# Layout conversion of four neighbourhood-attention outputs: spread over low-rank heads 3 to 6 instead of all at head 6

## The chip, the cores and the metric

The kernel runs on one core of one Trainium2 chip. A time is the device time of one execution in microseconds (us). A core has engines that work side by side, each through its own instructions in order: TensorE (PE, matrix products; its weight loads are shown as PEld), VectorE (DVE), ScalarE (ACT), GpSimd (POOL) and SyncE (SP), which here issues most of the transfers. Engines wait for each other by semaphores. On-chip tiles lie in SBUF, results of PE in PSUM banks.

## The reference, cut to what matters

Two layers of a diffusion backbone over 512 latent tokens (a grid 64 wide) and 256 context tokens, 1024 features. Layer 0 mixes two groups of eight heads each, low-rank (latent) attention and two-dimensional neighbourhood attention, and gives their concatenated outputs to one output projection:

```python
def even_mixer(...):
    ...
    o_mla_lat, o_mla_ctx = mla_heads(p_lat[..., :MLA_IN], p_ctx[..., :MLA_IN], rows, cols,
                                     q_norm, kv_norm, w_q_up, w_uk, w_uv, ctx_out)
    ...
    o_na_lat, o_na_ctx = na_heads(na_l[:, :, 0], na_l[:, :, 1], na_l[:, :, 2],
                                  na_c[:, :, 0], na_c[:, :, 1], na_c[:, :, 2], rel_bias, ctx_out)
    o_lat = jnp.concatenate([o_mla_lat, o_na_lat], axis=-1) @ w_out
    o_ctx = jnp.concatenate([o_mla_ctx, o_na_ctx], axis=-1) @ w_out if ctx_out else None
```

Then `h = h + g_a * o`, a SwiGLU block, and layer 1 (sliding-window attention, SwiGLU). The output is the final norm of the latent tokens. All of it is float32.

## The kernel before

Activations are kept with features on the 128 partitions and all 768 tokens along the row: columns 0 to 511 latent (`LATS`), 512 to 767 context (`CTXS`). A float32 product is made of three matmuls: each operand is split into a high part and the rest, and `mm3` (lines 335, 337, 338) multiplies high × high, high × rest and rest × high. `load_w` (line 319) brings a weight block: a transfer by SP into a `wr` buffer (three of them), the high part by ACT (line 324) into `wh`, the rest by DVE (line 325) into `wl`.

During attention the latent tokens are in an order by half-blocks of the grid. Neighbourhood heads run first, two heads to a pair, and each pair leaves one tile of 128 features × 768 tokens: the list `ON`, four tiles. The low-rank heads 0 to 7 follow, and their pairs leave four more: `OM`. Every pair's tile must be put back in rows of the grid and split into high part and rest before the output projection can use it. `in_rows` (line 1163) does both in one go, with four instructions: on ACT a copy of the latent columns (line 1168) and one of the context columns (1169), which give the high part; on DVE two subtractions (1170, 1171), which give the rest. This is called a conversion below. Conversions of `ON` write into general buffers (tag `b`), those of `OM`, at line 1209 behind the head loop, into buffers of tag `st`. So in the profile a row `b<-b` at line 1168 belongs to the neighbourhood outputs and `st<-b` to the low-rank ones.

One low-rank head is worked like this. PE makes scores (lines 1118 to 1120) into the three `pss` banks; DVE adds and finds the extreme (`take`, line 555) into a tile `p` (every fourth time one of the tag `wr`); ACT takes the exponential (551); PE transposes 128 × 128 blocks (499) into banks `pst` and `psd`; DVE (490) or ACT (491) moves them to SBUF as `ph` and `pl`; PE forms the weighted sums (545) in the one `pso` bank, and ACT copies them to the pair's tile (639). At the end of a pair the sums are inverted (475), spread over the partitions with two transposes (367), and multiplied in (`L482`, DVE). `latent_operands` prepares the next heads: a copy by ACT (1108) and a subtraction by POOL (1109).

The output projection (`output`, from line 1230) goes over eight blocks of 128 output features, first for columns 384 to 767 (`TOK2`), then for the others. For a block, 8 × 3 matmuls of 128 × 384 sum over the eight converted tiles: the four of `ON` first in the list `O`, then the four of `OM`. Its residual is loaded by eight transfers `in_xn` on SP (line 134).

The program is written in one order, and the framework's scheduler sets each engine's order at build time. It simulates a timeline, and takes for each engine the ready instruction with the first claim, by a priority that follows the order in which the instructions were written. So a call written earlier changes where its instructions and those around it stand. `attend` draws jobs from `mla_jobs` one ahead, and the lines after a head's `yield from` run when its jobs have been drawn.

Of the kernel before, what the change touches and what calls it, by code (L numbers as in the profile page):

```python
# [98 lines left out]
def hybrid_kernel(ctx: ExitStack, tc, I, out):  # L99
# [6 lines left out]
    def T(tag, shape, dt=F32):  # L106
        count[0] += 1
        if tag not in SIZES:
            return sb.tile(shape, dt, tag=tag, name=f"{tag}_{count[0]}", bufs=BUFS.get(tag, 1))
        n = int(np.prod(shape[1:]))  # L110
        t = sb.tile([P, SIZES[tag] // (2 if dt == mybir.dt.bfloat16 else 4)], dt, tag=tag, name=f"{tag}_{count[0]}",
                    bufs=BUFS[tag])[: shape[0], :n]
        if len(shape) == 3:
            t = t.rearrange("p (a b) -> p a b", a=shape[1])
        return t

    def B(dt=F32, tag="b"):
        return T(tag, [P, NT], dt)

    def PS(tag):  # L120
        count[0] += 1
        return ps.tile([P, 512], F32, tag=tag, name=f"ps{tag}_{count[0]}", bufs=PBUFS[tag])
# [13 lines left out]
    def f(ap):  # L136
        return ap.bitcast(F32) if ap.dtype == F32R else ap
# [219 lines left out]
    def split(src, eng=None, dst=None):  # L357

        p, n = src.shape
        h, lo = dst or (B(F32R), B(F32R))  # L360
        marks["cast"] = S.copy(h[:p, :n], src)  # L361
        marks["split"] = (eng or V).tensor_tensor(lo[:p, :n], src, f(h[:p, :n]), op=ALU.subtract)
        return h, lo
# [267 lines left out]
    def head_jobs(h, po, then):  # L631

        r = slice(64 * h.side, 64 * h.side + 64)
        for qs in ((4,), (5,)), ((0, 1), (2, 3)):

            def use(o, qs=qs):
                for i, x in enumerate(qs):
                    c = slice(x[0] * P, (x[-1] + 1) * P)
                    S.copy(po[r, c], o[64 * i : 64 * i + 64, : c.stop - c.start])

            yield job([(h, x) for x in qs], use, then if qs[0][0] == 0 else None)
# [20 lines left out]
    def drain(gen=None):  # L662

        while side_work and (gen is None or gen in side_work):
            step()
# [107 lines left out]
    def keys_of(v, side, mixed=None):  # L773

        def get(kt):
            t, i = (v, kt) if kt < 6 else (mixed, kt - 6)
            return t[:, i * P + 64 * side : i * P + 64 * side + 64]

        return get
# [156 lines left out]
    def beside(gen):  # L936
        side_work.append(gen)
        return gen
# [60 lines left out]
    ON, lat_raw, kr = [], [None] * 3, []  # L999
# [31 lines left out]
    def finish(po, sums, nq):  # L1031
        finish_pair(po, sums, nq)
        yield
# [35 lines left out]
    def pair_ups(p):  # L1069
        kn.append(B())  # L1070
        qn.append(B())
        wk = wu["kv"]
        yield from up(cut((wk[0][:, 0:1], wk[1][:, 0:1]), p * P, P), wu["ckv"], put(kn[p]))
        yield from up(cut(wu["qn"], p * P, P), wu["cq"], put(qn[p], scale=MLA_SCALE))
        if p % 2 == VP:
            yield from values(p - VP)
# [16 lines left out]
    def latent_operands(h):  # L1093
        p, s = divmod(h, 2)
        r, u = NOPE[s], USED[s]
        rr = slice(32 * (h % 4), 32 * (h % 4) + 32)
        if p < 2:
            if p == 0:
                KA.append([T("st", [P, NT], F32R) for _ in range(2)])
            QA[s].append([T("st", [P, NT], F32R) for _ in range(2)])  # L1100
            for t in [*(KA[s] if p == 0 else ()), *QA[s][p]] if s else ():
                (V if "z" in EV else G).memset(f(t[:32]), 0.0)
            if p == 0:
                for i in range(2):
                    V.tensor_copy(KA[s][i][ROPE[s]], KR[i][:32])
        (ka, kc), (qa, qb) = KA[s], QA[s][p % 2]
        for x, (hi, lo) in ((kn[p], (ka, kc)), (qn[p], (qa, qb))):
            S.copy(hi[r], x[r])
            (V if "l" in EV and p < 1 else G).tensor_tensor(lo[r], x[r], f(hi[r]), op=ALU.subtract)
        for t, x in zip((qa, qb), QR[h // 4]):  # L1110
            if "d" in EV:
                dma(t[ROPE[s]], x[rr])
            else:
                G.dma_start(t[ROPE[s]], x[rr])

        def scores(o, q, keys):
            q = slice(q * P, (q + 1) * P)
            PE.matmul(o, qa[u, q], ka[u, keys], start=True, stop=False)
            PE.matmul(o, qb[u, q], ka[u, keys], start=False, stop=False)
            PE.matmul(o, qa[u, q], kc[u, keys], start=False, stop=True)  # L1120

        return scores
# [40 lines left out]
    def in_rows(src, dst=None):  # L1163

        h, lo = dst or (B(F32R), B(F32R))
        half_blocks = lambda x: x[:, LATS].rearrange("p (n r c) -> p r n c", n=GW // HB, c=HB)
        rows = lambda x: x[:, LATS].rearrange("p (r n c) -> p r n c", n=GW // HB, c=HB)
        S.copy(rows(h), half_blocks(src))  # L1168
        S.copy(h[:, CTXS], src[:, CTXS])
        V.tensor_tensor(rows(lo), half_blocks(src), rows(f(h)), op=ALU.subtract)  # L1170
        V.tensor_tensor(lo[:, CTXS], src[:, CTXS], f(h[:, CTXS]), op=ALU.subtract)
        return h, lo


    OM, O = [], []

    def mla_jobs():
        phase[0], lower[0] = 1, LOWER
        rate[0] = STEPS[1], BG[0][4]
        ready.append(latent_operands(1))  # L1180
        for h in range(8):
            p, s = divmod(h, 2)
            if s == 0:
                g = beside(pair_ups(p + 1)) if p < 3 else None
                po = B()
                sums, mins = T("sm", [P, 6, 2]), T("sm", [P, 6, 2])
            yield from head_jobs(Head(s, ready[h], keys_of(VM[p], s), lambda n: (0, 4), lambda n: zeros.to_broadcast([P, NL]),
                                      -LOWEST, sums, mins), po, finish(po, sums, 6) if s else None)
            if s == 0 and g:
                drain(g)  # L1190
            if h < 6:
                ready.append(latent_operands(h + 2))
            if h == 6:
                O.extend(in_rows(o) for o in ON)
            if s == 1:
                OM.append(po)

    attend(mla_jobs())
    drain()
    dense[0] = True  # L1200
# [365 lines left out]
    for t0, n in ((0, 4), (4, 2)):  # L1566
        o = PS("t")
# [8 lines left out]
    OS, O = [], []  # L1576
# [36 lines left out]
    O = [split(o[:, LATS], dst=(B(F32R, "st"), B(F32R))) for o in OS]  # L1613
# [179 lines left out]
```

## Time and profile before

| | us |
|---|---|
| runs | 1585.27, 1585.99, 1589.26 |
| median | 1585.99 |
| profiled execution | 1587.13 |
| its span | 1585.4 |
| PE busy | 1531.6 (97% of the span) |
| DVE busy | 1163.0 (73%) |
| ACT busy | 796.2 (50%) |
| POOL busy | 294.7 (19%) |

The granted TensorE clock was 0.994 of full speed. The span runs from the first to the last instruction that the profiler recorded; the execution's own time has a little more around it. In what follows a stretch such as 366–372 is in microseconds from the start of the span. The low-rank heads' work lies before about 390, with the neighbourhood heads ahead of it; the output projection of layer 0 begins to be mixed into it near 370. A row of the timeline gives the start, the length, the engine, the line, the operation, out<-in, and, in brackets, how long the engine was idle before it and what released it. Rows of one line and form that follow each other are put together (x2, x4).

### The profile page before, as it was taken

What the parts mean: (1) busy time and instruction counts of PE and PEld (TensorE: products, weight loads), DVE (VectorE), ACT (ScalarE), POOL (GpSimd) and SP (SyncE); (2) the same over time, 40 slices, a digit from 0 to 9 for tenths busy, and PEclk for the clock granted to TensorE, in tenths of its full rate; (3) what the DMA queues carried; (4) which work ended last, traced back from release to release, by engine and by line L of the source; (5) the groups of instructions that cost most, each with busy time, mean ns of one, the idle gap of its engine ahead of it and who ended that gap; (6) DMA issues with size and microseconds to landing.
All of it is one profiled execution on the core that took longest, in us unless ns stands there. A gap on an engine that the chain in (4) does not pass through costs nothing. (4 is left out here: it accounts for less than half of the span.)

```text
span 1585.4 us, 26553 instructions
## 1 busy us (share of the span) xinstructions
PE 1531.6 (97%) x10024; PEld 1375.6 (87%) x10024; DVE 1163.0 (73%) x2331; ACT 796.2 (50%) x1607; POOL 294.7 (19%) x316
## 2 busy tenths in 40 slices
PE   6999999999999999999999999989999999999998
PEld 4787778877998999998989998878889998899997
DVE  3885787676677696887768666868876778678685
ACT  4563687675555242332323334557756545454453
POOL 0144634210011101111020221492012000000001
PEclk9999999999999999999999998999999999999999
DMA  9745332004444645547475585131015123324222
GB/s 311 253 130 175 86 119 72 16 2 160 165 156 142 197 146 192 189 123 276 139 268 171 173 322 181 42 98 49 1 48 167 54 97 124 103 84 131 88 89 87
DMA packets 76464, 214.91 MB, mean 136 GB/s; under 512 B 9872, under 2 KB 16400, under 8 KB 76336
## 3 DMA queue, kind: packets, MB, share of 16 engines
q1 hardware_dynamic: 59216, 144.42, 28.2%
q0 software_dynamic: 15968, 67.24, 12.3%
q8 instruction: 78, 1.28, 0.3%
q10 hardware_dynamic: 1152, 1.57, 0.3%
q14 instruction: 50, 0.41, 0.1%
HBM read 186.97 MB, written 23.07 MB: 132 GB/s over the span
## 5 line engine op out<-in xcount | busy, mean ns | idle before, releaser
L324 ACT CAST wh<-wr 128x1024 fp32r<-128x1024 f32 (+2 forms) x148 | 115.4, 795 | 207.1 <-PE pss L1377 33.8
L325 DVE TENSOR_TENSOR wl<-wr,wh 128x1024 fp32r<-128x1024 f32 (+2 forms) x145 | 135.5, 942 | 79.8 <-ACT wh L324 79.6
L551 ACT ACTIVATE p<-p,sm 128x512 f32<-128x512 f32 (+3 forms) x144 | 104.9, 729 | 27.1 <-DVE sm L555 25.3
L233 DVE CUSTOM_DVE_ANT_0 p<-rope,cond 128x1024 bf16<-128x1024 f32 x64 | 77.1, 1221 | 47.5 <-DMA rope<-in_mod_w_dram 47.5
L1378 PE MATMUL pss<-b,wl 128*128 128x384 f32 (+1 forms) x346 | 106.9, 312 | 1.7 <-DVE wl L1364 1.7
L1376 PE MATMUL pss<-b,wh 128*128 128x384 f32 (+1 forms) x346 | 107.7, 312 | 0.6 <-ACT b L361 0.6
L1377 PE MATMUL pss<-b,wh 128*128 128x384 f32 (+1 forms) x346 | 107.9, 312 | 0.1
L337 PE MATMUL psd<-b,wh 128*128 128x512 f32 (+3 forms) x262 | 89.7, 342 | 0.0
L335 PE MATMUL psd<-b,wh 128*128 128x512 f32 (+3 forms) x222 | 80.1, 361 | 1.6 <-ACT b L464 1.2
L338 PE MATMUL psd<-b,wl 128*128 128x512 f32 (+3 forms) x222 | 78.5, 355 | 0.0
L545 PE MATMUL pso<-ph,b 128*64 128x256 f32 (+1 forms) x384 | 77.2, 359 | 0.4 <-DVE ph L490 0.4
L545 PE MATMUL pso<-pl,b 128*64 128x256 f32 (+1 forms) x384 | 76.7, 359 | 0.7 <-DVE pl L490 0.7
L1378 PE MATMUL pst<-b,wl 128*128 128x384 f32 (+1 forms) x226 | 70.8, 313 | 3.0 <-DVE wl L1364 3.0
L228 POOL DMA_DIRECT2D rope<-in_mod_w_dram x48 | 25.5, 532 | 244.0 <-DVE mod L233 230.9
L1377 PE MATMUL pst<-b,wh 128*128 128x384 f32 (+1 forms) x226 | 70.5, 312 | 0.0
L1376 PE MATMUL pst<-b,wh 128*128 128x384 f32 (+1 forms) x226 | 70.5, 312 | 0.0
L337 PE MATMUL pss<-b,wh 128*128 128x256 f32 (+3 forms) x216 | 69.6, 322 | 0.1
L1659 POOL TENSOR_TENSOR p<-p,p 128x256 f32<-128x256 f32 x6 | 4.6, 766 | 347.3 <-ACT p L1655 347.2
L335 PE MATMUL pss<-st,wh 128*128 128x512 f32 (+2 forms) x198 | 67.3, 340 | 1.1 <-ACT st L1168 0.8
L1378 PEld LDWEIGHTS pss<-b,wl 128*128 128x128 f32 x346 | 65.4, 190 | 2.5 <-DVE wl L1364 2.2
L338 PE MATMUL pss<-st,wl 128*128 128x512 f32 (+2 forms) x198 | 67.1, 339 | 0.0
L1376 PEld LDWEIGHTS pss<-b,wh 128*128 128x128 f32 x346 | 65.6, 190 | 1.1 <-ACT b L361 0.9
(623 smaller groups left out, 5403.9 us busy)
## 6 DMA issues: line engine op xcount, KB each, us to landing
wr<-in_w_gu_dram SPq DMA_DIRECT2D x88, 512.0 KB, 4.2
rope<-in_mod_w_dram POOLq DMA_DIRECT2D x48, 512.0 KB, 3.8
wr<-in_w_dn_dram SPq DMA_DIRECT2D x73, 256.0 KB, 2.9
wr<-in_w_out_dram SPq DMA_DIRECT2D x32, 512.0 KB, 3.5
p<-home POOLq DMA_DIRECT2D x40, 384.0 KB, 5.4
home<-p POOLq DMA_DIRECT2D x40, 384.0 KB, 4.9
wr<-in_w_in_dram SPq DMA_DIRECT2D x21, 512.0 KB, 4.6
nb<-in_nb_dram SPq DMA_DIRECT2D x16, 384.0 KB, 3.3
```

The costliest lines, as they stand in the source:

```text
L228: G.dma_start(w, I["mod_w"][at])
L233: V.tensor_tensor_reduce(out=T("p", [P, D], mybir.dt.bfloat16), in0=w, in1=cond[:, v, :], op0=ALU.mult, op1=ALU.add, scale=1.0, scalar=0.0 ...
L324: behind(S.copy(h, r), *after[:1])
L325: behind((G if eng else V).tensor_tensor(lo, r, f(h), op=ALU.subtract), *after[1:])
L335: ins = PE.matmul(o, wh[:, k], mh[:, c], start=first and k == 0, stop=False)
L337: PE.matmul(o, wh[:, k], ml[:, c], start=False, stop=False)
L338: PE.matmul(o, wl[:, k], mh[:, c], start=False, stop=last and k == n - 1)
L545: ins = PE.matmul(o[64 * i : 64 * i + 64, c], v(kt), t, start=n == 0, stop=n == len(moving[i]) - 1)
L551: S.activation(p[:, c], p[:, c], AF.Exp, bias=nm, scale=-1.0, accum_out=dn)
L1376: PE.matmul(o, wh, xh, start=first and k == 0, stop=False, skip_group_check=not first)
L1377: PE.matmul(o, wh, xl, start=False, stop=False, skip_group_check=not first)
L1378: PE.matmul(o, wl, xh, start=False, stop=k == 3, skip_group_check=not first)
```

## The change

`mla_jobs` no longer converts all four neighbourhood outputs once head 6 has been drawn. It converts one after each of heads 3, 4, 5 and 6, in the list's order.

```diff
             if h < 6:
                 ready.append(latent_operands(h + 2))
-            if h == 6:
-                O.extend(in_rows(o) for o in ON)
+            if h in (3, 4, 5, 6):
+                O.append(in_rows(ON[len(O)]))
             if s == 1:
                 OM.append(po)
```

The instructions are the same in number and kind. Their order differs in one piece of the program, from head 3 to the start of the output projection.

VectorE, from the end of head 6 into head 7. `b_1822`, `b_1997`, `b_2290` and `b_2627` are the four neighbourhood outputs, `wl_4304` and `wl_4340` the rests of the second and third weight block. Before:

```order
L490 COPY ph_4064<-pst_4059 128x512
L475 RECIPROCAL sm_4202<-sm_3846 128x12
L1170 TENSOR_TENSOR b_4000<-b_1997,b_3999 128x512
L1171 TENSOR_TENSOR b_4000<-b_1997,b_3999 128x256
L1170 TENSOR_TENSOR b_4006<-b_2290,b_4005 128x512
L1171 TENSOR_TENSOR b_4006<-b_2290,b_4005 128x256
L490 COPY ph_4107<-pst_4102 128x512
L325 TENSOR_TENSOR wl_4304<-wr_4301,wh_4303 128x1024
L1170 TENSOR_TENSOR b_4012<-b_2627,b_4011 128x512
L1171 TENSOR_TENSOR b_4012<-b_2627,b_4011 128x256
L490 COPY ph_4158<-psd_4153 128x512
L325 TENSOR_TENSOR wl_4340<-wr_4337,wh_4339 128x1024
```

Now:

```order
L490 COPY ph_4064<-pst_4059 128x512
L475 RECIPROCAL sm_4202<-sm_3864 128x12
L490 COPY ph_4107<-pst_4102 128x512
L490 COPY ph_4158<-psd_4153 128x512
L490 COPY pl_4165<-pst_4160 128x512
L325 TENSOR_TENSOR wl_4304<-wr_4301,wh_4303 128x1024
L490 COPY ph_4172<-pst_4167 128x512
L490 COPY ph_4186<-pst_4181 128x512
L325 TENSOR_TENSOR wl_4340<-wr_4337,wh_4339 128x1024
```

Six subtractions are gone from here. The two weight subtractions stand behind more copies of head 7 than before: `wl_4304` behind `ph_4158` and `pl_4165`, `wl_4340` behind all of them. On TensorE the first block's products up to the last finished low-rank pair now stand together ahead of head 7's first sums; before, most of them came behind these.

ScalarE, at head 5. `b_3528` before and `b_3534` now are the same pair's tile. Before:

```order
L551 ACTIVATE p_3806,sm_3529<-p_3806,sm_3530 128x768
L551 ACTIVATE wr_3825,sm_3529<-wr_3825,sm_3530 128x768
L639 COPY b_3528<-pso_2914 64x128 x2
L1108 CAST st_2915<-b_3552 64x768
L1168 CAST st_4240<-b_3182 128x512
L1169 CAST st_4240<-b_3182 128x256
L551 ACTIVATE p_3835,sm_3529<-p_3835,sm_3530 128x768
```

Now:

```order
L639 COPY b_3534<-pso_2914 64x128 x2
L1168 CAST b_3716<-b_1997 128x512
L1169 CAST b_3716<-b_1997 128x256
L1108 CAST st_2915<-b_3558 64x768
L1168 CAST st_4240<-b_3182 128x512
L1169 CAST st_4240<-b_3182 128x256
L551 ACTIVATE wr_3837,sm_3535<-wr_3837,sm_3536 128x768
L1168 CAST b_3857<-b_2290 128x512
L1169 CAST b_3857<-b_2290 128x256
L551 ACTIVATE p_3847,sm_3535<-p_3847,sm_3536 128x768
```

The second and third neighbourhood output are converted here, the second ahead of the operands' copy (1108) that POOL waits for, the third between two exponentials. The pair of low-rank heads 2 and 3 (`st_4240`) was converted here before too.

TensorE, behind the last head's last weighted sums (`pso_2914`); `pss_4343` is the third output block. Before:

```order
L545 MATMUL pso_2914<-ph_4158,b_3282 64x256
L545 MATMUL pso_2914<-pl_4151,b_3282 64x256
L367 MATMUL pst_4212<-ident_r_86,pl_4213 128x128 x2
L335 MATMUL pss_4343<-st_4240,wh_4339 128x384
L337 MATMUL pss_4343<-st_4241,wh_4339 128x384
L338 MATMUL pss_4343<-st_4240,wl_4340 128x384
L335 MATMUL pss_4343<-st_4246,wh_4339 128x384
L337 MATMUL pss_4343<-st_4247,wh_4339 128x384
L338 MATMUL pss_4343<-st_4246,wl_4340 128x384
L335 MATMUL pss_4272<-st_4252,wh_4268 128x384
```

Now:

```order
L545 MATMUL pso_2914<-ph_4158,b_3282 64x256
L545 MATMUL pso_2914<-pl_4151,b_3282 64x256
L338 MATMUL pss_4343<-b_3528,wl_4340 128x384
L335 MATMUL pss_4343<-b_3716,wh_4339 128x384
L337 MATMUL pss_4343<-b_3717,wh_4339 128x384
L367 MATMUL pst_4212<-ident_r_86,pl_4213 128x128 x2
L338 MATMUL pss_4343<-b_3716,wl_4340 128x384
L335 MATMUL pss_4343<-b_3857,wh_4339 128x384
L337 MATMUL pss_4343<-b_3858,wh_4339 128x384
L338 MATMUL pss_4343<-b_3857,wl_4340 128x384
L335 MATMUL pss_4343<-b_4011,wh_4339 128x384
```

Six products of the third block stood between the last head and the first product that needs its converted output (`st_4252`); now 19 do, eight of them in the rows shown; `b_3528`, `b_3716`, `b_3857` and `b_4011` are here the high parts of the four neighbourhood outputs. On SP, the eight loads `in_xn`, which stood behind the third load of `w_out`, now stand between the first and the second.

## The prediction

> **What bounds the kernel now.** I read the page first: busy time by engine, then the chain that ended last.
>
> ```profile
> span 1585.4 us, 26553 instructions
> PE 1531.6 (97%) x10024; PEld 1375.6 (87%) x10024; DVE 1163.0 (73%) x2331; ACT 796.2 (50%) x1607; POOL 294.7 (19%) x316
> PE 31%; DVE 3%; issue 3%; DMA 3%; POOL 2%; ACT 1%; DVEq 0%; POOLq 0%; ACTq 0%
> ```
>
> PE is busy 97% of the span and holds most of what the chain shows. The change adds and removes no instruction, so it can only win back PE's waits. They total 53.8 us over the whole span (1585.4 − 1531.6), and few of them are near the edit. So I read busy time by stretch next (columns: stretch, length, then PE, PEld, DVE, ACT and POOL busy, PE clock, DMA share, GB/s).
>
> ```profile
> 340.00:350.00 10.00, 9.28 (x69) 7.10 (x69) 8.77 (x23) 6.18 (x16) 1.83 (x1) 1.00 0.00 2
> 366.00:372.00 6.00, 4.37 (x27) 2.76 (x26) 6.00 (x11) 5.98 (x14) 0.00 (x0) 1.00 0.32 87
> 390.00:400.00 10.00, 8.28 (x44) 6.13 (x41) 7.60 (x14) 5.96 (x10) 0.00 (x0) 1.00 0.14 29
> ```
>
> Two places matter. In 366–372, after head 6, where all four conversions stand, DVE (6.00 of 6) and ACT (5.98) are full and PE is short by 1.63 us. In 390–400, where the low-rank heads hand over to the output projection, PE is short by 1.72 us. At 340–350, where two of the conversions go, DVE has 1.23 us left.
>
> **The change, part by part. The price of one conversion.** ACT's timeline around head 6 (start, length, instruction, the wait before it in brackets); `b<-b` rows at L1168 and L1169 are conversions of neighbourhood outputs, `st<-b` rows those of low-rank outputs, which stay:
>
> ```profile
> 366.13 0.62 ACT L1168 CAST b<-b 128x512 fp32r<-128x512 f32 x1
> 366.96 0.62 ACT L1168 CAST st<-b 128x512 fp32r<-128x512 f32 x1
> 369.66 0.61 ACT L1168 CAST b<-b 128x512 fp32r<-128x512 f32 x1
> 370.59 0.59 ACT L491 COPY pl<-pst 128x512 f32<-128x512 f32 x1
> ```
>
> From one conversion's start to the next instruction's, 366.13 to 366.96, is 0.83 us of ACT. DVE's timeline there:
>
> ```profile
> 368.46 0.68 DVE L1170 TENSOR_TENSOR b<-b,b 128x512 fp32r<-128x512 f32 x1
> 369.39 0.68 DVE L1170 TENSOR_TENSOR st<-b,st 128x512 fp32r<-128x512 f32 x1
> 370.33 0.68 DVE L490 COPY pl<-psd 128x512 f32<-128x512 f32 x1
> 370.93 1.21 DVE L325 TENSOR_TENSOR wl<-wr,wh 128x1024 fp32r<-128x1024 f32 x1
> ```
>
> By the same reading, 368.46 to 369.39 is 0.93 us of DVE. Three of the four leave: 3 × 0.83 = 2.5 us of ACT and 3 × 0.93 = 2.8 us of DVE. The fourth output (`ON[3]`) is still converted after head 6, just where the first one stood, so up to about 370 us both engines run as before.
>
> **Term 1, start of the tail.** PE's timeline:
>
> ```profile
> 367.40 0.33 PE L499 MATMUL pst<-ident_r,wr 128*128 128x128 f32 x1 [0.58 <-DVE ph L490]
> 371.07 0.65 PE L545 MATMUL pso<-pl,b 128*64 128x256 f32 x2 [0.71 <-DVE pl L490]
> 372.13 0.60 PE L499 MATMUL pst<-ident_r,p 128*128 128x128 f32 x4
> 372.49 0.42 PE L338 MATMUL pss<-b,wl 128*128 128x384 f32 x1
> ```
>
> The four transposes at 372.13 (0.36 us until L338 starts) need the PSUM bank that ACT's L491 copy at 370.59 empties. That copy stands behind a departing conversion (369.66, until 370.59). Without it the transposes fit into the 0.71 us gap ahead of 371.07, and L338 starts at about 372.13, held then by DVE's L325 (370.93 + 1.21 = 372.14). Gain 0.36; bounds 0 and 0.71, the whole gap. The earlier wait of 0.58 stays, since DVE's rows ahead of it are the same.
>
> **Term 2, end of the tail.** The last low-rank head's output takes a copy, a normalisation and its own conversion before PE may use it (timelines of PE, ACT and DVE):
>
> ```profile
> 390.48 0.38 PE L545 MATMUL pso<-pl,b 128*64 128x256 f32 x1
> 390.79 0.44 PE L367 MATMUL pst<-ident_r,pl 128*128 128x128 f32 x2
> 391.94 0.34 PE L338 MATMUL pss<-st,wl 128*128 128x384 f32 x1
> 393.08 0.44 PE L335 MATMUL pss<-st,wh 128*128 128x384 f32 x1 [0.80 <-ACT st L1168]
> ...
> 390.91 0.74 ACT L639 COPY b<-pso 64x256 f32<-64x256 f32 x2 [5.94 <-PE pso L545]
> ...
> 391.34 1.04 DVE L482 TENSOR_TENSOR b<-b,pst 128x256 f32<-128x256 f32 x2 [6.57 <-PE pst L367]
> ...
> 392.41 0.62 ACT L1168 CAST st<-b 128x512 fp32r<-128x512 f32 x1 [0.17 <-DVE b L482]
> ```
>
> From the last L545 at 390.48 this takes until 392.41 + 0.62 = 393.03, so 2.55 us. Behind that L545, PE now has two L367 and six products; the sixth, at 391.94, would be followed at one product's spacing, 0.18 us ((391.94 − 390.79 less some 0.25 for the two L367) / 5), at 392.12. PE stands from 392.12 to 393.08: 0.96 us. In the changed order 19 products of output block 2 and the two L367 stand there: 19 × 0.18 + 0.25 = 3.7 us, more than 2.55, so the chain is covered. Gain 0.96; bounds 0 (if those products wait themselves) and 0.96.
>
> **Term 3, a new wait in the tail.** DVE's subtraction for the second weight block (`wl_4304`) moves behind the copy of four of head 7's transposes (`pl_4165`), and PE wants it soon after these:
>
> ```profile
> 378.19 0.66 PE L545 MATMUL pso<-ph,b 128*64 128x128 f32 x8
> ```
>
> DVE needs 0.60 for the copy (370.33 to 370.93) and 1.21 for the subtraction (370.93), together 1.81, from the transposes' end. PE has two products, these sums (0.6) and two groups of four transposes (0.36 each) ahead of the L338 that reads it: 2 × 0.18 + 0.6 + 0.72 = 1.7. Queued behind that L338 is all of the second block. The difference is 0.1, and the hand-over from PE to DVE comes on top; if the copy's 0.60 counts whole it is 0.6. Bounds 0 and −0.60; I take −0.3, the middle.
>
> **Term 4, heads 4 and 5 (340–347 us).** Two conversions (`ON[1]`, `ON[2]`) come here, into this piece:
>
> ```profile
> 344.50 0.50 PE L1118 MATMUL pss<-st,st 96*128 96x512 f32 x1 [0.72 <-DVE sm L555]
> 345.80 0.30 PE L499 MATMUL psd<-ident_r,wr 128*128 128x128 f32 x1
> ...
> 342.50 0.94 ACT L551 ACTIVATE p<-p,sm 128x768 f32<-128x768 f32 x1
> ...
> 342.83 1.27 DVE L1170 TENSOR_TENSOR st<-b,st 128x512 fp32r<-128x512 f32 x1
> 344.03 0.41 DVE L555 CUSTOM_DVE_ANT_0 p<-pss,zeros 128x256 f32<-128x256 f32 x1
> ```
>
> PE stands 0.72 for a score take, L555 at 344.03, that sits behind a 1.27 us subtraction. The new order has that take ahead of the pair's subtraction, at about 343.0 to 343.3, so 0.72 comes free. Against that, the two exponentials of this block now stand behind two conversions on ACT, 2 × 0.83 = 1.66 us: the one that ended at 342.50 + 0.94 = 343.4 would end near 345.1, with the queue's other moves near 345.6. PE's transposes of it, at 345.80 now, would come at 345.80 − 0.72 = 345.08 if free, and so wait some 0.5. Net +0.2. Bounds: +0.72 if the exponentials come in time, and −1.0 if the 1.66 counts in full (0.72 − 1.66).
>
> **Term 5, after head 3 (309–311 us).** One conversion, `ON[0]`. Its cover:
>
> ```profile
> 313.38 0.83 ACT L1108 CAST st<-b 64x768 fp32r<-64x768 f32 x1 [1.50 <-PE pss L1119]
> ...
> 312.18 0.42 DVE L555 CUSTOM_DVE_ANT_0 wr<-pss,zeros 128x256 f32<-128x256 f32 x1 [0.46 <-PE pss L1120]
> ```
>
> ACT is idle 1.50 before 313.38, against 0.83 added: covered. DVE has 0.46 idle against 0.93, so about 0.5 of the take at 312.18 may be late; PE is then behind other products for that long. I take 0, bounds 0 and −0.47.
>
> **Term 6, SP's queue.** The eight residual loads move ahead of the second weight load:
>
> ```profile
> 368.02 0.33 SPq L134 DMA_DIRECT2D wr<-in_w_out_dram  x1
> 372.55 5.65 SPq L134 DMA_DIRECT2D b<-in_xn_dram  x8
> 394.28 2.94 ACT L324 CAST wh<-wr 128x1024 fp32r<-128x1024 f32 x3 [1.26 <-PE pss L337]
> ```
>
> They issue 5.65 us in total. Their buffers are free once the second conversion's subtraction has run (about 342), so they go out behind the first weight load, with the DMA nearly idle (0.00 in 340–350), and are done before the second load's issue at 368.02, which waits for its slot in any case. Later weight loads no longer stand behind them. The casts at 394.28 wait for PE to release a buffer, not for a transfer, so nothing shortens: 0.
>
> **Sum.** 0.36 + 0.96 − 0.3 + 0.2 = 1.2 us gained. After 394 the instruction order is the same and each wait is on work already shifted, so the 1.2 passes to the end. The profiled execution took 1587.13 us for its span of 1585.4, so 1585.9; it lies 1.14 above the median of the runs, 1585.99. On that median the forecast is **1584.8 us**. Lowest and highest of the bounds together: 0.71 + 0.96 + 0.72 = 2.4 gained; 0.60 + 1.0 + 0.47 = 2.1 lost.
>
> **The rivals.**
>
> **A, slower: POOL holds DVE's subtraction.** The same conversion's subtraction takes 0.68 at 368.46 but 1.27 at 342.83, and 1.92 at 329.24. What ran beside it on POOL:
>
> ```profile
> 329.24 1.92 DVE L1170 TENSOR_TENSOR st<-b,st 128x512 fp32r<-128x512 f32 x1 [0.77 <-ACT st L1168]
> ...
> 328.76 1.85 POOL L1109 TENSOR_TENSOR st<-b,st 64x768 fp32r<-64x768 f32 x1 [12.62 <-ACT st L1108]
> 341.72 1.83 POOL L1109 TENSOR_TENSOR st<-b,st 64x768 fp32r<-64x768 f32 x1 [4.13 <-ACT st L1108]
> ```
>
> POOL ends at 330.61 and 343.55; DVE's two ends are 331.16 and 344.10, both 0.55 later, as if DVE only began when POOL was done. In the change, ACT's L1108, which starts POOL's L1109, stands right behind `ON[1]`'s copies; its subtraction should start at 341.0 to 342.3 and POOL at 341.75 to 342.5, a margin of 0.1 to 0.4 us. It decides from the point where POOL starts first: then DVE is held about 1.9. DVE in 340–350 would need 8.77 + 2 × 0.93 + 1.9 − 0.6 (the hold that it has today) = 11.9 of 10 us, so PE comes out 1.9 late there; less terms 1 to 3 (1.02) that is 0.9 lost, 1586.9. For it: the margin is thin. Against it: the order puts the subtraction first. The Trainium skill, "SBUF — State Buffer", section "SBUF: two separate sides", says a DVE operation with two SBUF inputs and a GpSimd operation that reads SBUF take a shared port pair as an exclusive lock, the one that starts second blocked to the end. By that rule the hold is the whole 1.83 and not a share; the trace agrees (both ends 0.55 after POOL's).
>
> **B, a larger gain: the jam after head 6 clears.** PE lacks 1.63 in 366–372 and 0.96 at 392. If the 2.5 and 2.8 us taken from ACT and DVE let nearly all of it go, with term 4's 0.72 and no loss, it is 3.3, so 1582.7. For it: both engines are full there. Against it: the rows up to 370 stay. The Trainium skill, "Perfetto Trace Analysis", section "Identifying the Most-Contended Engine", holds matmul busy time a bad measure of how near a kernel is to the limit and weight-load busy time a good one. By it PE has more to spare than 97% says, as PEld's 2.76 of 6 agrees; this speaks for B.
>
> **C, nothing: what the tail gains is given back** by the late exponentials of term 4 at their bound of −1.0 (1.02 − 1.0 = 0.02): 1586.0.
>
> **How the numbers follow.** Forecast (0.5 to 2.2 gained) 0.48; C 0.25; A 0.14; B 0.13. What a measurement can tell from no change is about 0.3%, 4.8 us: faster is below 1581.2, slower above 1590.8. Forecast and C lie inside. B reaches below 1581.2 only with other waits gone too: I give 0.05 of its 0.13 to that. A reaches above 1590.8 if the hold repeats at heads 3 and 5 and is passed on: 0.04 of its 0.14. So same is 0.91. The range: from B's 1582.7 less 0.5 for the runs' own spread to A's 1586.9 plus 0.9 for one more half hold: 1582.2 to 1587.8. The forecast's own range is 1583.8 to 1585.5.
>
> **What would show it.** Term 1: L499 transposes ahead of the L545 near 371, L338 no later than 372.2. Term 2: no wait on L1168 of `st` before the first L335 of the last pair. Term 3: a wait of PE on DVE's wl of up to 0.6 near 380. Term 4: the wait on L555 near 344 gone, one on the exponential near 345 of about 0.5. A: L1170 `b<-b` of about 1.9 near 341, its end 0.55 behind POOL's. Term 5: no new PE wait at 309–314. Term 6: the residual loads issued before 366. The forecast is wrong if PE's busy time in 340–350 falls below 8.5, or if a wait appears after 394 that is not there today.

## The result, and the profile after

| | kernel before | changed kernel |
|---|---|---|
| median (16 runs each) | 1588.26 us | 1582.69 us |
| lowest to highest | 1581.54 to 1590.69 | 1577.93 to 1588.01 |
| ratio | | 0.9969, 95% interval [0.9957, 0.9981] |
| ratio, a second comparison | | 0.9981 [0.9967, 0.9996] |
| ratio, a third comparison | | 0.9992 [0.9976, 1.0009] |
| profiled execution's span | 1585.4 | 1578.0 |

The changed kernel is a little faster: the three comparisons give 0.31%, 0.19% and 0.08%, and the last interval reaches past 1. The forecast was a gain of 1.2 us, 0.08%. The runs of one program are spread over 10 us, so times alone can't tell 1.2 us from 5; the traces can, because the part of the program that the change touches takes the same time in every execution, to 0.01 us in the changed kernel and 0.24 us in the kernel before. I measure that part between two instructions that stand in all versions in the same place: TensorE's transposes after a wait of 0.19 us on line 464, and the third product in a row that waits for `wh`. Two more instructions that the prediction named divide it: the transposes behind the wait of 0.58 us, and the first L338 of the output projection. TensorE's timeline of the kernel before (the two inner rows, at 367.40 and 372.49, stand in the prediction):

```profile
252.80 0.66 PE L499 MATMUL psd<-ident_r,p 128*128 128x128 f32 x4 [0.19 <-ACT b L464]
...
397.28 0.44 PE L335 MATMUL psd<-b,wh 128*128 128x384 f32 x1 [0.33 <-ACT wh L324]
```

The same in the changed kernel:

```profile
251.09 0.66 PE L499 MATMUL psd<-ident_r,p 128*128 128x128 f32 x4 [0.19 <-ACT b L464]
...
344.00 0.33 PE L499 MATMUL psd<-ident_r,p 128*128 128x128 f32 x1 [0.61 <-ACT p L551]
...
365.27 0.33 PE L499 MATMUL pst<-ident_r,wr 128*128 128x128 f32 x1 [0.58 <-DVE ph L490]
...
368.94 0.65 PE L545 MATMUL pso<-pl,b 128*64 128x256 f32 x2
...
370.07 0.44 PE L338 MATMUL pss<-b,wl 128*128 128x384 f32 x1
...
390.01 0.33 PE L335 MATMUL pss<-st,wh 128*128 128x384 f32 x1
...
393.90 0.45 PE L335 MATMUL psd<-b,wh 128*128 128x384 f32 x1 [0.34 <-ACT wh L324]
```

The changed kernel reaches this part 1.71 us earlier (251.09 against 252.80), before anything has changed; that is chance (its other two traces reach it at 254.28 and 256.05, those of the kernel before at 256.11 and 256.26). Then:

| us | heads 0 to 6 | start of the tail | end of the tail | sum |
|---|---|---|---|---|
| before (three traces) | 114.60, 114.61, 114.60 | 5.09, 5.09, 5.09 | 24.79, 24.80, 25.03 | 144.48, 144.50, 144.72 |
| changed (three traces) | 114.18, 114.18, 114.18 | 4.80, 4.80, 4.79 | 23.83, 23.83, 23.83 | 142.81, 142.81, 142.80 |
| gain | 0.42 | 0.29 | 0.96 | 1.67 |

Three of before's waits have gone: 0.72 at 344.50, 0.71 at 371.07 (the L545 at 368.94 has no bracket), 0.80 at 393.08 (nor has the first product of the last pair, at 390.01). One has come that costs time, 0.61 on an exponential at 344.00. (A wait of 0.21 on an exponential at 367.68 costs nothing: that row starts 2.41 us behind the one with the wait of 0.58 in both kernels.) Busy time in the three stretches of the prediction, each 1.7 us earlier:

```profile
338.30:348.30 10.00, 9.39 (x73) 7.40 (x71) 9.54 (x28) 7.16 (x18) 1.99 (x1) 1.00 0.01 2
364.30:370.30 6.00, 4.90 (x29) 2.96 (x28) 6.00 (x12) 4.88 (x9) 0.00 (x0) 1.00 0.50 160
388.30:398.30 10.00, 9.06 (x49) 8.00 (x48) 7.50 (x13) 4.89 (x9) 0.00 (x0) 1.00 0.27 98
```

TensorE: 9.39 for 9.28, 4.90 for 4.37, 9.06 for 8.28. ScalarE has lost 1.10 us of work after head 6 (4.88 for 5.98), while VectorE is still full there (6.00).

### The profile page after: what moved, and what is told of

Same layout as the page of the kernel before. It is cut to its first block, busy times and chain, and to the rows that moved or that the text cites. A ratio compares the mean times of both kernels' runs of the same rounds, so it can differ in the third digit from the quotient of the medians.

```text
span 1578.0 us, 26546 instructions
## 1 busy us (share of the span) xinstructions
PE 1528.9 (97%) x10024; PEld 1373.9 (87%) x10024; DVE 1161.7 (74%) x2331; ACT 795.9 (50%) x1607; POOL 294.5 (19%) x316
## 5 line engine op out<-in xcount | busy, mean ns | idle before, releaser
L325 DVE TENSOR_TENSOR wl<-wr,wh 128x1024 fp32r<-128x1024 f32 (+2 forms) x145 | 135.6, 943 | 82.8 <-ACT wh L324 81.2
L338 PE MATMUL psd<-b,wl 128*128 128x512 f32 (+3 forms) x222 | 78.8, 356 | 0.0
L545 PE MATMUL pso<-ph,b 128*64 128x256 f32 (+1 forms) x384 | 77.5, 360 | 0.4 <-DVE ph L490 0.2
L545 PE MATMUL pso<-pl,b 128*64 128x256 f32 (+1 forms) x384 | 76.5, 359 | 0.0
L338 PE MATMUL pss<-st,wl 128*128 128x512 f32 (+2 forms) x198 | 67.1, 339 | 0.0
```

The source lines that it names most:

```text
L325: behind((G if eng else V).tensor_tensor(lo, r, f(h), op=ALU.subtract), *after[1:])
L338: PE.matmul(o, wl[:, k], mh[:, c], start=False, stop=last and k == n - 1)
L545: ins = PE.matmul(o[64 * i : 64 * i + 64, c], v(kt), t, start=n == 0, stop=n == len(moving[i]) - 1)
```

## The experiments

The theory that I tested (L below) is the prediction's: the change acts in this part alone, by its terms 1, 2 and 4. Against it stood rival B (the jam after head 6), rival A (POOL holding VectorE), and D: the lead or the buffers that come free also remove waits further on, in the SwiGLU. "The stretch" is, in expectations that give it 115 to 119 us, the one from VectorE's row at 308 to its row at 427 (118.7 us in before); where they give 174 to 178, it is the one from TensorE's row at 250 to its row at 427 (176.95 in before), which is 58.2 us longer. I give the second, and the first where an expectation needs it. Both change between versions as the sum in the table above does, by 1.67 us for the change. The edits shown are against the changed kernel, unless another is named.

### Both kernels again

Nothing is edited in these four runs.

> The kernel before, once more, as a second trace of the same program and as a null for the timing. Theory L (all that the change does lies between 294 and 414 us, and the rest of the difference between the two profiles is chance of the transfers): time ratio 1.000 within 0.002; the waits of 0.72, 0.71 and 0.80 us at 344, 371 and 393 stand here again to 0.05, but PE's waits on weights in the first SwiGLU (3.8 us of waits on line 1364 in 600 to 900 before, 1.8 less in the profile of the change) move by 1 us or more in this repeat. Theory D (the change also removes waits for weights in the SwiGLU): these waits return within 0.4 us of 3.8.

> The changed kernel once more. Both theories: the stretch from 294 to 414 us comes out 1.5 to 1.8 us shorter than before's, with one new wait of 0.5 to 0.7 on an exponential near 344. L: time 0.998 to 0.9995 of the kernel before (1 to 3 us less), SwiGLU waits on line 1364 between 1.5 and 4.5 us. D: time 0.996 to 0.998 (3 to 6 us less), and these waits at about 2.0, as in the first profile of the change.

> The kernel before, a third trace. Stretch from 250 to 427: 176.9 to 177.0. What lies outside that stretch took 1408.4 and 1409.8 us in its two traces, 1402.8 to 1410.3 in the eight of other versions. Theory L (outside, only chance): anywhere from 1402 to 1411, ratio 0.998 to 1.002. Theory D (the kernel before is longer outside as well): 1408 to 1411.

> The changed kernel, a third trace. Stretch from 250 to 427: 175.2 to 175.3. Outside it 1402.8 and 1407.6 us in its two traces. Theory L: anywhere from 1402 to 1411; time against the third copy of the kernel before in this same call 1 to 3 us less. Theory D: 1402 to 1407 and 4 to 6 us less.

| | stretch | span less stretch | ratio to the kernel before |
|---|---|---|---|
| before, first trace | 176.95 | 1408.4 | |
| before_again | 176.99 | 1409.8 | 0.999 [0.9974, 1.0007] |
| before_third | 177.19 | 1412.9 | 0.9996 [0.9979, 1.0013] |
| changed, first trace | 175.28 | 1402.8 | 0.9969 [0.9957, 0.9981] |
| after_again | 175.28 | 1407.6 | 0.9981 [0.9967, 0.9996] |
| after_third | 175.29 | 1407.9 | 0.9992 [0.9976, 1.0009] |

The stretch repeats to 0.01 us in the changed kernel and to 0.24 in the kernel before. What lies outside it moves by 5 us between executions of one program, with the same instructions in the same order. So most of the 7.4 us between the first two spans was no effect of the change. D's narrow form, that the SwiGLU waits come back as they were, fails: TensorE's wait on `wl` of line 1364 at 658 us, 0.72 in the first trace of before, is gone in its second. But L missed too: the waits on that line between 600 and 900 moved by 0.9 (3.8 to 2.9), where it asked for 1 or more, and the third trace of before, 1412.9 outside the stretch, lies above the range of both. Whether the part outside is a little longer in the kernel before all the same is not settled. Its three values, 1408.4 to 1412.9, are high: of the eight from other versions (1402.9 to 1410.4) only one exceeds the lowest of them. Its waits on line 1364, 3.8, 2.9 and 3.4, all lie above the changed kernel's 1.8, 2.6 and 1.6, with 0.9 to 3.0 in the other versions. Against it stand the times: the kernel before against itself came out at 0.999 and 0.9996, a scatter as large as what would have to be told apart. One piece of it, 0.65 us at the very end, is systematic; it is told in the last section.

### One conversion moved

```diff
-            if h in (3, 4, 5, 6):
-                O.append(in_rows(ON[len(O)]))
+            for o in {3: ON[:1], 6: ON[1:]}.get(h, ()):
+                O.append(in_rows(o))
```

> Only the first neighbourhood output is converted early, after head 3; three stay at head 6. L by its terms: the wait at 344 us stays (0.72, since nothing moves there), the end of the tail still gains if enough products stand behind the last sums (0 to 0.96), so 0 to 1.3 us less than before: 0.999 to 1.000. D: if any early release of buffers or any lead into the SwiGLU brings the later gain, 2.5 us or more less: below 0.9985.

Stretch 178.32, 1.37 us *longer* than before; ratio 1.0007 [0.9992, 1.0022]. The miss teaches most about rival A. POOL's, VectorE's and TensorE's timelines at head 5:

```profile
339.05 1.84 POOL L1109 TENSOR_TENSOR st<-b,st 64x768 fp32r<-64x768 f32 x1 [2.75 <-ACT st L1108]
...
339.70 1.73 DVE L1170 TENSOR_TENSOR st<-b,st 128x512 fp32r<-128x512 f32 x1 [0.62 <-issue]
...
342.09 0.33 PE L499 MATMUL pst<-ident_r,wr 128*128 128x128 f32 x1 [1.06 <-DVE ph L490]
```

POOL starts first, VectorE's subtraction takes 1.73 in place of 0.69 and ends 0.54 after POOL, and the copy queued behind it keeps TensorE waiting for 1.06. In the changed kernel the conversion of `ON[1]` stands ahead of POOL's operands and prevents just this. The end of the tail had its cover (two L367 and 21 products behind the last sums) and no wait, as expected; but the scheduler put the subtraction of `ON[1]` ahead of a copy of head 6, and the wait of 0.58 became 1.49.

### Three conversions left out

The first three neighbourhood outputs are not converted; the projection reads the fourth one's conversion in their place.

```diff
-            if h in (3, 4, 5, 6):
-                O.append(in_rows(ON[len(O)]))
+            if h == 6:
+                O.extend([in_rows(ON[3])] * 4)
```

> The conversions of the first three neighbourhood outputs are left out, and the fourth output's conversion is read in their place (the output is not the reference's). 2.5 us of ScalarE and 2.8 us of VectorE are gone altogether. L: against the changed kernel only the cost of the placed conversions is left to gain, the 0.6 us wait on the exponential near 344 and what is hidden: the stretch 294 to 414 is 2.0 to 2.9 us shorter than before's, time 1.5 to 4 us less than before (0.9975 to 0.999). Rival B (the jam after head 6 is what costs): the stretch is 3.3 us or more shorter.

Ratio 0.9989 [0.9973, 1.0005], stretch 175.70: 1.25 less than before, and 0.42 *more* than in the changed kernel, which does all the work. TensorE's timeline:

```profile
254.81 0.65 PE L499 MATMUL psd<-ident_r,p 128*128 128x128 f32 x4 [0.19 <-ACT b L464]
...
346.51 0.50 PE L1118 MATMUL pss<-st,st 96*128 96x512 f32 x1 [0.72 <-DVE sm L555]
...
369.41 0.33 PE L499 MATMUL pst<-ident_r,wr 128*128 128x128 f32 x1 [0.58 <-DVE ph L490]
...
374.21 0.44 PE L338 MATMUL pss<-b,wl 128*128 128x384 f32 x1
...
398.04 0.45 PE L335 MATMUL psd<-b,wh 128*128 128x384 f32 x1 [0.33 <-ACT wh L324]
```

Its parts are 114.60, 4.80 and 23.83: the heads as before, with the wait of 0.72 back, the tail exactly as in the changed kernel. So the tail's gain is 0.29 + 0.96 = 1.25, all that comes of taking these three conversions from there. Rival B, 3.3 us, is out. L's 2.0 to 2.9 is missed as well: it took for granted that the wait of 0.72 would stay away without the conversions that reorder heads 4 and 5. With them, and the order that comes with them, the heads take 0.42 less than without: in their new places the three conversions cost nothing on balance.

### One at head 3, one at head 4, two at head 6

```diff
-            if h in (3, 4, 5, 6):
-                O.append(in_rows(ON[len(O)]))
+            for o in {3: ON[:1], 4: ON[1:2], 6: ON[2:]}.get(h, ()):
+                O.append(in_rows(o))
```

> One conversion after head 3, one after head 4, and two after head 6 (in the change: one after each of heads 3 to 6). It is the change with one conversion moved back, so that it stands on ScalarE ahead of the L491 copy again, and no longer between two exponentials at head 5. Theory, term by term: the wait of 0.61 us on an exponential at 345.8 goes; the wait of 0.71 us near 371 on the copies comes back (term 1 is that copy's place behind a conversion); no wait at the end (two L367 and 17 rows stand behind the last sums). The stretch from PE's row at 250 to its row at 427 us, 176.97 in before and 175.28 in the change, takes 175.0 to 175.5. Rival to term 1: if the wait near 371 came from the sum of the work there and not from this copy, it comes back by a part only, and the stretch takes 174.7 or less.

Stretch 175.09, ratio 0.9976 [0.9962, 0.9991]. ScalarE's and TensorE's timelines:

```profile
367.02 0.60 ACT L1168 CAST b<-b 128x512 fp32r<-128x512 f32 x1
367.53 0.40 ACT L1169 CAST b<-b 128x256 fp32r<-128x256 f32 x1
367.96 0.59 ACT L491 COPY pl<-pst 128x512 f32<-128x512 f32 x1
...
250.83 0.66 PE L499 MATMUL psd<-ident_r,p 128*128 128x128 f32 x4 [0.19 <-ACT b L464]
...
364.76 0.33 PE L499 MATMUL pst<-ident_r,wr 128*128 128x128 f32 x1 [0.58 <-DVE ph L490]
...
368.43 0.65 PE L545 MATMUL pso<-pl,b 128*64 128x256 f32 x2 [0.71 <-DVE pl L490]
...
369.85 0.42 PE L338 MATMUL pss<-b,wl 128*128 128x384 f32 x1
...
393.45 0.44 PE L335 MATMUL psd<-b,wh 128*128 128x384 f32 x1 [0.33 <-ACT wh L324]
```

With one conversion again ahead of ScalarE's copy, the wait of 0.71 is back in full, and the first L338 comes 5.09 behind the transposes as in the kernel before, not 4.80. That is term 1 by itself: 0.29. The wait on the exponential is gone (heads 0 to 6 take 113.93, 0.25 less than in the change), and the end of the tail takes 23.60. The sum is 142.62, 0.19 less than the changed kernel: the shortest stretch of all versions, but by less than the times can tell.

### One head earlier each

```diff
-            if h in (3, 4, 5, 6):
+            if h in (2, 3, 4, 5):
```

> The four conversions one head earlier each: after heads 2, 3, 4 and 5. In this order no product at all stands between the last head's L367 and the first product that needs its converted output (six in before, 19 with two L367 in the change). Theory of term 2 (those products are what covers the last head's chain of copy, normalisation and conversion, 2.55 us from the last L545): PE stands about 2.0 us on L1168 of the st tile there (2.55 less 0.31 and 0.25), though ScalarE and VectorE have less to do after head 6 than in any other version; the stretch that took 118.7 us before (from 308 to 427) takes 117.9 to 118.9. Rival B (the work after head 6 is what costs): no wait there, 116.5 or less.

Stretch 177.22 (119.00 from 308, just above the 117.9 to 118.9 expected), ratio 0.9983 [0.9964, 1.0002]. TensorE's timeline:

```profile
338.53 0.50 PE L1118 MATMUL pss<-st,st 128*128 128x512 f32 x1 [1.14 <-DVE sm L555]
...
369.21 0.33 PE L499 MATMUL pst<-ident_r,wr 128*128 128x128 f32 x1 [0.58 <-DVE ph L490]
...
373.07 0.44 PE L338 MATMUL pss<-b,wl 128*128 128x384 f32 x1
...
392.46 0.44 PE L367 MATMUL pst<-ident_r,pl 128*128 128x128 f32 x2
394.74 0.44 PE L335 MATMUL pss<-st,wh 128*128 128x384 f32 x1 [1.84 <-ACT st L1168]
```

With no product left between the last head and its converted output, TensorE stands for 1.84 us, against 0.80 in before and 0 in the change; 2.0 was expected. No version has less work after head 6, so it is the products behind the last sums, and not the work taken away, that cover the chain. The wait of 1.14 at 338.53 comes with the POOL hold once more, at another head (a subtraction of line 1170 takes 2.03 there).

The version also shows what the conversion that stayed behind head 6 costs. The start of the tail takes 3.86 (369.21 to 373.07), 0.94 less than in the change. VectorE's timeline there:

```profile
370.26 0.68 DVE L1170 TENSOR_TENSOR st<-b,st 128x512 fp32r<-128x512 f32 x1
...
371.20 0.68 DVE L490 COPY pl<-psd 128x512 f32<-128x512 f32 x1
```

The copy that TensorE's L545 waits for starts 1.99 behind the transposes of 369.21, where in the change it starts 2.93 behind them (368.20 against 365.27): it stands behind one pair of subtractions and not two, and one pair was priced at 0.93. So the one conversion in front of this copy costs 0.94, and the change leaves one there.

### Heads 2, 3, 4 and 6, and the operands on VectorE

```diff
-            if h in (3, 4, 5, 6):
+            if h in (2, 3, 4, 6):
```

> Two conversions go to heads 2 and 3, one stays ahead of POOL's operands at head 4, none at head 5, one at head 6. Theory: the new wait of 0.61 us on an exponential at 345.8 goes, since only one conversion stands ahead of it; 26 or more products stand behind the last sums, so no wait there; the stretch takes 116.3 to 116.8 us (117.06 in the change), time 0.6 less than the change, 2.3 less than before (0.9985). Rival A (POOL holds VectorE): one L1170 in 300 to 350 takes 1.2 us or more beside POOL where it now takes 0.69, and the stretch is 117.5 or more.

Stretch 175.33 (117.11 from 308, for the 116.3 to 116.8 expected), ratio 0.998 [0.9962, 0.9997]. The wait on the exponential went as expected, and rival A came instead. POOL's, VectorE's and TensorE's timelines:

```profile
334.19 5.97 POOL L1109 TENSOR_TENSOR st<-b,st 64x768 fp32r<-64x768 f32 x3 [14.45 <-ACT st L1108]
...
336.43 2.03 DVE L1170 TENSOR_TENSOR st<-b,st 128x512 fp32r<-128x512 f32 x1 [0.87 <-POOL st L1109]
...
340.83 0.50 PE L1118 MATMUL pss<-st,st 128*128 128x512 f32 x1 [1.14 <-DVE sm L555]
```

Is it POOL's running that holds VectorE? The next run is the kernel before with one operation on another engine:

```diff
-            (V if "l" in EV and p < 1 else G).tensor_tensor(lo[r], x[r], f(hi[r]), op=ALU.subtract)
+            V.tensor_tensor(lo[r], x[r], f(hi[r]), op=ALU.subtract)
```

> The kernel before, with POOL's operand subtraction (line 1109) on VectorE. Rival A's mechanism: if POOL's running is what lengthens VectorE's subtraction, L1170 of the st tiles near 329 and 343 takes 0.69 us, not 1.92 and 1.27. If the form or the stride of these is what is slow, they stay over 1.2.

VectorE's timeline of its one execution, which has no ratio:

```profile
337.57 0.68 DVE L1170 TENSOR_TENSOR st<-b,st 128x512 fp32r<-128x512 f32 x1
...
348.14 0.69 DVE L1170 TENSOR_TENSOR st<-b,st 128x512 fp32r<-128x512 f32 x1
```

Without POOL the same two subtractions take 0.68 and 0.69, not 1.92 and 1.27, so POOL was the cause of their length. The wait of 0.72 at 344 is gone too, and the stretch is 176.17, 0.8 less than before; but the order moved with the edit (against the transposes with the wait of 0.58, the two subtractions start 5.8 and 2.8 us later than before), so POOL's share in that wait is not shown by itself. Then both edits together:

> Conversions after heads 2, 3, 4 and 6, and the operands' subtraction (line 1109) on VectorE in place of POOL. Theory (POOL's running held VectorE's subtraction of 2.03 us at 336 and so made PE's wait of 1.14): both go, every L1170 takes 0.69, and the stretch from 250 to 427 takes 174.0 to 174.8 us (175.33 with POOL, 175.28 in the change, 176.97 before). Rival: VectorE's extra work (16 x 0.95 us) makes new waits of as much: 175.2 or more. Time 0.998 to 0.9985 of the kernel before if the first holds.

Every L1170 took 0.69, as expected, but the stretch is 178.07, longer than before, and the ratio 1.0003 [0.9989, 1.0017]: the rival's time came. Two of its new waits in TensorE's timeline:

```profile
313.86 0.33 PE L499 MATMUL psd<-ident_r,wr 128*128 128x128 f32 x1 [0.65 <-ACT b L491]
...
346.08 0.33 PE L499 MATMUL psd<-ident_r,wr 128*128 128x128 f32 x1 [0.61 <-ACT wr L551]
```

Both end on ScalarE, on a copy and an exponential. The edit changed the order on the other engines as well, so that VectorE's extra work itself makes these waits, as the rival has it, is not shown.

### Heads 1 to 4

```diff
-            if h in (3, 4, 5, 6):
+            if h in (1, 2, 3, 4):
```

> All four conversions after heads 1 to 4, so none is left at heads 5 and 6; 20 rows stand behind the last sums, so the chain is covered. Theory: no exponential wait of 0.61, no wait at the end, and 0.8 to 0.9 us less on ScalarE and VectorE after head 6 (the waits of 0.58 and 0.21 there shrink by 0 to 0.6): stretch 115.8 to 116.8, 0.998 to 0.9985 of before. Rival: the earlier heads (309 to 340) have no such room and a wait of 0.5 or more appears there: 117.0 or more.

Stretch 177.56, or 0.6 longer than before where 1.9 to 2.9 less was expected, ratio 0.9995 [0.9977, 1.0013]: the rival again. The wait of 1.14 near 340 comes with the POOL hold as before (2.03 for the subtraction), and waits of 0.24 and 0.68 are new near 288, where the first conversion now stands. By the stretch, no version with a conversion at head 1 or 2 beats the change.

## Why the prediction was right, point by point

It said a small gain, 1584.8, in a range of 1582.2 to 1587.8. The measured median, 1582.69, lies near the range's lower end, and the direction is right. That this median falls inside, and on rival B's 1582.7, is luck: against the 1588.26 of the kernel before in the same comparison it is a gain of 5.6 us, more than the 2.4 of all the bounds together, of which the traces show 2.3 (1.67 here, 0.65 at the program's end). The forecast is borne out by the stretch, which gained 1.67 us where the sum was 1.2, and by its parts:

- **Term 1, the copy behind a conversion: 0.36 forecast, 0.29 measured** (5.09 to 4.80). L338 now starts right behind L325 on VectorE, as written. The rows in the changed kernel, with those of terms 3, 4 and 6:

```profile
368.80 1.22 DVE L325 TENSOR_TENSOR wl<-wr,wh 128x1024 fp32r<-128x1024 f32 x1
...
378.06 1.22 DVE L325 TENSOR_TENSOR wl<-wr,wh 128x1024 fp32r<-128x1024 f32 x1
...
379.33 0.45 PE L338 MATMUL psd<-b,wl 128*128 128x384 f32 x1
...
339.67 0.69 DVE L1170 TENSOR_TENSOR b<-b,b 128x512 fp32r<-128x512 f32 x1
340.27 0.42 DVE L1171 TENSOR_TENSOR b<-b,b 128x256 fp32r<-128x256 f32 x1
...
343.34 0.42 DVE L555 CUSTOM_DVE_ANT_0 p<-pss,zeros 128x256 f32<-128x256 f32 x1
...
340.40 1.99 POOL L1109 TENSOR_TENSOR st<-b,st 64x768 fp32r<-64x768 f32 x1 [3.44 <-ACT st L1108]
...
342.93 0.93 ACT L551 ACTIVATE p<-p,sm 128x768 f32<-128x768 f32 x1
...
354.81 3.76 SPq L134 DMA_DIRECT2D b<-in_xn_dram  x8
```

L325 ends at 370.02 and L338 starts at 370.07. The L545 that had the wait of 0.71 starts 3.67 behind the transposes with the wait of 0.58 in both kernels: the four transposes moved into the gap ahead of it, as forecast.
- **Term 2, the cover behind the last sums: 0.96 forecast, 0.96 measured** for the end of the tail as a whole (24.79 to 23.83), and no wait at 390.01.
- **Term 3, the new wait on the second weight block: −0.3 forecast, none measured.** This is the step that was mis-sized. VectorE's subtraction ends at 379.28 and L338 starts at 379.33, directly behind TensorE's transposes: the two come out level. I had set 1.81 us of VectorE against 1.7 of TensorE, a difference of 0.1, and then took the middle of the bounds. The two sums themselves were the better estimate.
- **Term 4, heads 4 and 5: 0.2 forecast, 0.42 measured.** The wait of 0.72 went and one of 0.61 came (0.5 forecast), on the exponential that ends at 343.86 behind two conversions. The waits account for 0.11; the other 0.31 lies in rows without a wait over 0.1 us. TensorE's products stand in another order there, and I can't assign it.
- **Terms 5 and 6: 0 and 0.** TensorE has no new wait over 0.1 us before 344, and the residual loads went out at 354.81 to 358.57, before 366, with no one waiting for them.
- **Rival A** was a true mechanism with the wrong place. In the change VectorE's subtraction starts at 339.67, 0.73 ahead of POOL, and takes 0.69. In four other versions POOL came first; VectorE was then held to 1.73 or 2.03, and TensorE's wait was 1.06 to 1.14, not the 1.9 that A was priced at. By the Trainium skill, "SBUF — State Buffer", section "SBUF: two separate sides", whichever of such a pair starts first keeps the ports for its whole instruction; the traces agree where POOL is first. Where VectorE is first they agree in direction: POOL's operation, which starts 0.13 behind L1171, takes 1.99 against its usual 1.84, 0.15 longer, though L1171 had 0.29 left.
- **Rival B** fell with the conversions left out (1.25, not 3.3). The reading behind it was wrong: in 366–372 not all four conversions stand. Of VectorE's subtractions only the first output's do; the next starts later, in the kernel before at

```profile
372.80 0.62 DVE L1170 TENSOR_TENSOR b<-b,b 128x512 fp32r<-128x512 f32 x1
```

so taking three away left VectorE as full there as it was (6.00 of 6). B's jam was real, but for the most part it hung on the conversion that stayed: in the version with heads 2 to 5, which moves that one too, 0.94 more came free.
- **Rival C** asked for 1.0 lost at head 5; the wait there is 0.61 and the net is a gain.
- The chance of 0.05 for faster by over 0.3% was low for a measurement with this spread: the first comparison came out at 0.31%, with an interval of 0.19 to 0.43%. The 2.3 us that the traces show (1.67, and 0.65 below), 0.15%, lie within the intervals of the second and third comparison and just outside the first. What lies between is open.

## What to carry to other kernels

Where TensorE is full, ask of every moved step what it stands in front of in its new queue: here 2.5 us of ScalarE's work off a crowded place was worth 0.29 us through the one copy that stood behind it, another 0.96 came because 19 products, not six, then stood behind the last sums, and the one conversion that cost 0.94 was left where it was. Cover a late chain with products that depend on nothing in it, and count them. When runs spread over 10 us, compare a change of 1 us between two instructions of the trace that stand on either side of it.

## What was not expected of the hardware

The program ends about 0.65 us sooner after its last VectorE work in the changed kernel, though nothing was changed there. The last row of the chain of waits, of before and of the changed kernel:

```profile
1579.72 1.96 DVE p L1649 x5
```

```profile
1573.10 1.96 DVE p L1649 x5
```

From the end of this work to the end of the span it is 3.72 us in before (1585.4 − 1581.68; 3.54 and 3.55 in its other traces, 3.65 in the version with one conversion moved), and 2.94 in the change (1578.0 − 1575.06; 2.93 and 2.98), 2.87 with one, one and two, and 2.80 to 3.01 in the other versions. The DMA queues between 1580 and 1584 in before (packets, MB, share of 16 engines):

```profile
q10 hardware_dynamic: 576, 0.52, 40.0%
q1 hardware_dynamic: 513, 0.46, 35.1%
q14 instruction: 1, 0.01, 0.5%
```

One load of instructions falls among the last stores there, as it does in before's other two traces and with one conversion moved; in the change, the same four microseconds hold no such load. With one, one and two there is a load, but it comes when the last packet of the stores has moved, and the end is not late. In before some 15 packets of the stores still move more than 1.5 us after the VectorE work's end, in the change none. I take it that the load delays the packets queued behind it on its DMA engine. That is argued from the traces; no run tested it, and why the load falls there in some versions and not in others stays open.
